# A hybrid decoder layer on one core: another order of seven-product and plain chunk pairs in its feed-forward parts, and padded pools

## The chip, the cores and the metric

One core of a Trainium2 chip runs the whole layer in one launch. The metric is the time of one execution on the device in microseconds. TensorE (PE) multiplies matrices, VectorE (DVE) and ScalarE (ACT) work elementwise, GpSimd (POOL) does little here, and SyncE (SP) issues the loads and stores. On-chip memory (SBUF) has 128 partitions; an address below is a byte offset within a partition. Matmul results go into eight accumulation banks (PSUM), each 512 float32 values wide per partition.

## The reference

The layer works on 256 tokens of width 2048 in float32:

```
x = x + 1/2 * SwiGLU_1(RMSNorm(x))            # 2048 -> 5632 -> 2048
h = RMSNorm(x); u = h @ W_in
x = x + W_out [ GLA_group(u) ; MoBA_group(u) ]
x = x + CrossAttn(RMSNorm(x), RMSNorm(mem))   # 4 heads, memory of 256
x = x + 1/2 * SwiGLU_2(RMSNorm(x))

def swiglu(h, w_gate, w_up, w_down):
    return (jax.nn.silu(h @ w_gate) * (h @ w_up)) @ w_down
```

The change concerns the gate and up products of the two SwiGLU parts, and where tiles lie.

## The kernel before

Every float32 operand is split into a high part in the matmul format and a rest (`split_to`, L151 to L153: ScalarE copies to `hi`, VectorE subtracts to `lo`). A product is then three matmuls into one bank (`mm3`, L163 to L167): high by high, high of the activations by rest of the weights, rest of the activations by high of the weights. The stationary operand is a 128x128 block of activations, the moving one 512 columns of weights. One such triple is called a product here.

The tokens make two tiles of 128 (t = 0, 1), the width 2048 makes 16 chunks of 128. The feed-forward width 5632 makes 11 column blocks of 512. `ffn` (L404) goes through them in groups of 4, 4 and 3 blocks; after each group a down stage multiplies what the group made with `w_down`, in four blocks of 512 output columns. Block 0 runs its gate and its up product one after the other (`Block`). All other blocks, 10 in each of the two feed-forward parts, run gate and up together as a `Pair` (from L197).

A pair takes the 16 chunks two by two, in eight steps. `KINDS` gives each step's kind. In an N step (plain) the two token tiles and the two weight matrices are multiplied with four products per chunk, 8 in all, or 24 matmuls: banks p2, q4, r3, r5 in that order, where r3 takes the difference of the two token tiles (tiles dh, dl). In an S step the two chunks, two token tiles and two matrices are treated as a 2x2 matrix product with seven products, or 21 matmuls, over combinations of activations (tiles eh, el, made once by `Normed.sums`) and of weights: VectorE first forms combinations of the weights (L232 wide, L234 and L235 narrow, tiles `st`), and these are split like the weights themselves. So an S step has four split tiles (two from `raw`, two from `st`) and an N step two. The split tiles `whi` and `wlo` have six buffers each (`HIS`), the raw weights three (`RAWS`, one buffer for a step of a pair).

All S steps also add to p1, r6 and r7, which no N step uses. After the last S step `early` (L246) reads those three. At a pair's end `gates` and `ups` read p2, q4, r5, r3 and r5 again, ScalarE applies the silu, VectorE multiplies (L449), and `turn` transposes the result on TensorE and splits it, pumped between the steps of what follows. The seven banks are taken by the next pair in the order p1, r6, r7, p2, r5, r3, q4.

The order of instructions on each engine is fixed when the kernel is built: a scheduler orders them by priority and readiness and places the waits, so neighbouring steps are interleaved. Each engine then runs its own queue in order.

Tiles come from pools laid one behind the other, with sizes in multiples of 32 bytes per partition: const, wp (raw), act (x, xhi, xlo, bighi, biglo), small, then the phase's tmp (whi, wlo, t2k, xg, st and others) and own (eh, el, dh, dl in the feed-forward phases; m_cum, m_tail, m_ch, s8d, go, s8a, s8b, s8c, s4a, decay, s4b in the mixer's). In small stand 13 tags of two 32-byte buffers each.

The first lines on the order of work at a pair's end:

```
for t, (g, u) in enumerate(zip(list(pair.gates()), list(pair.ups()))):
    r = a.rstd[:, t:t + 1]
    nc.scalar.activation(g, g, AF.Silu, scale=r)
    nc.vector.scalar_tensor_tensor(u, u, r, g, op0=ALU.mult, op1=ALU.mult)
```

Of the kernel before, what the change touches and what calls it, by code (L numbers as in the profile page):

```python
# [9 lines left out]
F32 = mybir.dt.float32  # L10
F32R = mybir.dt.float32r
BF16 = mybir.dt.bfloat16
AF = mybir.ActivationFunctionType
ALU = mybir.AluOpType
# [3 lines left out]
P = 128  # L18
# [4 lines left out]
KC = D // P  # L23
# [4 lines left out]
GH = 4  # L28
# [7 lines left out]
NCH = T // CH  # L36
# [9 lines left out]
RAWS = 3  # L46
HIS = 6
T2K = 7
KINDS = "SSSSNNNN"


@with_exitstack
def hymba_layer(ctx: ExitStack, tc: tile.TileContext, x, mem, ffn1_norm, ffn1_w_gate, ffn1_w_up,
# [3 lines left out]
    nc = tc.nc  # L57
# [6 lines left out]
    const = ctx.enter_context(tc.tile_pool(name="const", bufs=1))  # L64
    wp = ctx.enter_context(tc.tile_pool(name="wp", bufs=RAWS))
    act = ctx.enter_context(tc.tile_pool(name="act", bufs=1))
    small = ctx.enter_context(tc.tile_pool(name="small", bufs=2))
    pools = {}
# [13 lines left out]
    def nm(s):  # L82
        count[0] += 1
        return f"{s}_{count[0]}"
# [1 line left out]
    x_sb = act.tile([P, NT, D], F32, tag="x", name="x_sb")  # L86
    norms = [ffn1_norm, mix_norm, xattn_norm, mem_norm, ffn2_norm]
    G1, GMIX, GX, GMEM, G2 = range(5)
    graw = const.tile([KC, P], F32, name="graw")
    nc.sync.dma_start(x_sb[:, :, :NB], x[:, :NB].rearrange("(t p) n -> p t n", p=P))  # L90
    nc.sync.dma_start(graw, ffn1_norm.rearrange("o (c p) -> (o c) p", p=P))
    warm = small.tile([P, 1], F32, tag="mx", name="warm")
    nc.vector.memset(warm, 0.0)
    nc.scalar.activation(warm, warm, AF.Silu)
    ident = const.tile([P, P], F32, name="ident")
# [1 line left out]
    gT1 = const.tile([P, 32], F32, name="gT1")[:, :KC]  # L97
# [4 lines left out]
    def turn_gains(src, dst):  # L102
        n = src.shape[0]
        ps = aux_tile([P, NB])
        nc.tensor.transpose(ps[:, :n], src, ident[:n, :n])
        nc.vector.tensor_copy(dst, ps[:, :n])

    def aux_tile(shape):
        n = 1
        for s in shape[1:]:  # L110
            n *= s
        t = pools["aux"].tile([P, NB], F32, tag="aux", name=nm("aux"))[:, :n]
        if len(shape) == 3:
            t = t.rearrange("p (a b) -> p a b", a=shape[1])
        return t
# [4 lines left out]
    def own_tile(shape, tag, dtype=F32):  # L120
        return pools["own"].tile(shape, dtype, tag=tag, name=nm(tag))

    def tmp_tile(shape, tag, bufs=2, dtype=F32):
        return pools["tmp"].tile(shape, dtype, tag=tag, name=nm(tag), bufs=bufs)

    def half_kb(shape=(P, NB)):
        return tmp_tile(list(shape), "t2k", 8 if "mix" in pools else T2K)
# [27 lines left out]
    def split_raw(raw):  # L155

        k, n = raw.shape[1:]
        bufs = 3 if "mix" in pools else HIS
        hi, lo = (tmp_tile([P, 2, NB], tag, bufs, F32R)[:, :k, :n] for tag in ("whi", "wlo"))
        split_to(hi, lo, raw)  # L160
        return [(hi[:, i, :], lo[:, i, :]) for i in range(k)]
# [7 lines left out]
    def bank(n=NB):  # L169
        return pools["mm"].tile([P, NB], F32, tag="mm", name=nm("mm"))[:, :n]  # L170
# [26 lines left out]
    class Pair:  # L197
# [3 lines left out]
        def __init__(self, a, wg, wu, c0):  # L201
            self.a, self.wg, self.wu, self.c0 = a, wg, wu, c0
            self.p = {n: bank() for n in ("p1", "r6", "r7", "p2", "r5", "r3", "q4")}
            self.left = {n: KINDS.count("S") + (0 if n in ("p1", "r6", "r7") else 1) *
                         KINDS.count("N") for n in self.p}
            self.total = dict(self.left)
# [11 lines left out]
        def step(self, q):  # L218
# [4 lines left out]
            g, u2 = raw[:, 1:3], raw[:, 3:4]  # L223
            if KINDS[q] == "N":
                gs, us = split_raw(g), split_raw(raw[:, 0:4:3])
# [36 lines left out]
        def ups(self):  # L262

            c = self.v2
            nc.vector.tensor_tensor(c, self.p["r5"], c, op=ALU.add)  # L265
            nc.vector.tensor_tensor(c, self.p["r3"], c, op=ALU.add)
            yield c
            c = self.v3
            nc.vector.tensor_tensor(c, self.p["r5"], c, op=ALU.add)  # L269
            yield c  # L270
# [3 lines left out]
    def pump():  # L274

        while behind:
            try:
                next(behind[0])
                return
            except StopIteration:  # L280
                behind.popleft()
# [60 lines left out]
    class Normed:  # L342
# [6 lines left out]
        def begin(self):  # L349
            self.hi, self.lo = (act_tile([P, KC, T], tag, F32R) for tag in ("xhi", "xlo"))  # L350
            self.ss = small.tile([P, NT, 4], F32, tag="ss", name=nm("ss"))
            if self.pairs:
                self.s = [q for q in range(KC // 2) if KINDS[q] == "S"]
                self.n = [q for q in range(KC // 2) if KINDS[q] == "N"]
                self.e = [own_tile([P, len(self.s), 4, P], t, F32R) for t in ("eh", "el")]
# [13 lines left out]
        def sums(self, q, x):  # L369

            f = tmp_tile([P, 4, P], "xg", 3)
            if KINDS[q] == "S":
                for out, x0, x1 in ((f[:, 0], x[1][:, 0], x[1][:, 1]),
# [97 lines left out]
        phases.append(phase(name, n_mm))  # L471
        phases[0].__enter__()

    turn_gains(graw, gT1)
    n1 = Normed(G1, True)

    def load_x(j):
# [13 lines left out]
    n1.block(0)  # L491
    behind.append(start())
    pump()
    graw2 = const.tile([4 * KC + 4, P], F32, name="graw2")
    for i, g in enumerate(norms[1:]):
        nc.sync.dma_start(graw2[i * KC:(i + 1) * KC, :], g.rearrange("o (c p) -> (o c) p", p=P))
    for i, g in enumerate((moba_q_norm, moba_k_norm, xattn_q_norm, xattn_k_norm)):
# [19 lines left out]

    m_cum = pools["own"].tile([P, P], F32R, name="m_cum")
    m_tail = pools["own"].tile([P, P], F32R, name="m_tail")
    m_ch = pools["own"].tile([P, 2], F32R, name="m_ch")  # L520
    mask = tmp_tile([P, P], "at", 4)
    nc.gpsimd.memset(mask, 1.0 / TAU)
    nc.gpsimd.affine_select(out=mask, in_=mask, compare_op=ALU.is_ge, fill=0.0, base=0,
# [25 lines left out]
    rg = own_tile([P, NT, GW], "s8b")  # L549
    qkT = own_tile([P, 2, GH, T], "s8c")  # L550
    ktail = own_tile([P, NT, GQK], "s4a")
    decay = own_tile([P, GH, NCH], "decay")
    E = {}

    def scaled(dst, ps, rstd):
# [451 lines left out]
```

## Time and profile before

| what | value |
|---|---|
| median of 3 runs (lowest to highest) | 1985.28 us (1985.1 to 1986.78) |
| the profiled execution's own time | 1984.34 us |
| its span in the trace | 1982.6 us |
| TensorE busy, matmuls | 1945.7 us, 8872 |
| VectorE busy, instructions | 1489.4 us, 1832 |
| ScalarE busy, instructions | 1047.5 us, 1308 |
| DMA | 369.12 MB, 55.4% of 16 engines' span |

Busy time is the time in which at least one instruction of an engine is in progress. Matmuls overlap: one lasts some 390 ns by its record and the next starts before it ends, so the distance of two starts is what a matmul costs in a stream. In rows of instructions a name stands as line, engine, operation, what it writes and what it reads; brackets give the idle time before it and what ended it.

### The profile page before, as it was taken

To read this page: it belongs to the slowest core of one execution; us is meant where nothing else is said; L and a number is where in the kernel's file an instruction comes from. 1 tells how busy PE (TensorE), PEld (TensorE's weight loads), DVE (VectorE), ACT (ScalarE), POOL (GpSimd) and SP (SyncE) were. 2 spreads that over 40 slices of the span, in tenths; PEclk is the share of its full clock that TensorE was granted. 3 is DMA by queue.
4 is the path that set the end of the run, shared out by engine and by line. 5 is a ranking of instruction groups with operands and counts; after the bars stand their busy time and mean duration, and the time that the engine had idled before them with its cause. 6 is when DMAs were issued, how large, how long until landed. Compare 5 with 4: busy or idle time off the path is not lost.

```text
span 1982.6 us, 23399 instructions
## 1 busy us (share of the span) xinstructions
PE 1945.7 (98%) x8872; PEld 1590.8 (80%) x8872; DVE 1489.4 (75%) x1832; ACT 1047.5 (53%) x1308; POOL 23.5 (1%) x52
## 2 busy tenths in 40 slices
PE   7999999999999999999999999999999999999999
PEld 6877887778887788987788888887788777888777
DVE  8898579995699755465665766989857999569973
ACT  6555446554355545635464645655534655435552
POOL 0000000000000000000000000000000000000000
PEclk9999999999999999999999999999999999999999
DMA  7555555565555636554456545655554566555563
GB/s 255 191 191 191 192 169 191 195 213 200 177 186 186 223 129 207 164 191 149 150 169 205 178 149 167 196 198 183 192 199 161 191 206 213 196 170 191 191 213 127
DMA packets 192456, 369.12 MB, mean 186 GB/s; under 512 B 8692, under 2 KB 19144, under 8 KB 192344
## 3 DMA queue, kind: packets, MB, share of 16 engines
q1 hardware_dynamic: 192344, 367.64, 55.4%
q8 instruction: 69, 1.13, 0.2%
q14 instruction: 43, 0.35, 0.1%
HBM read 365.50 MB, written 2.10 MB: 185 GB/s over the span
## 4 chain that ended last, share of the span: by engine, by line
PE 77%; DVE 17%; ACT 3%; issue 2%; DMA 1%; SPq 0%; ACTq 0%
PE mm L165 24%; PE mm L167 24%; PE mm L166 24%; DVE wlo L153 8%; ACT whi L152 3%; DVE st L232 2%; DVE st L235 2%; DVE st L234 1%; DVE biglo L153 1%; DVE t2k L449 1%; PE aux L328 1%; DVE t2k L256 0%; DVE t2k L265 0%; DVE t2k L269 0%; DVE t2k L259 0%
## 5 line engine op out<-in xcount | busy, mean ns | idle before, releaser
L153 DVE TENSOR_TENSOR wlo<-raw,whi 128x1024 fp32r<-128x1024 f32 (+3 forms) x704 | 796.3, 1142 | 377.1 <-ACT whi L152 375.1
L152 ACT ACTIVATE whi<-raw 128x1024 fp32r<-128x1024 f32 (+3 forms) x704 | 683.5, 989 | 661.6 <-PE mm L167 561.1
L165 PE MATMUL mm<-whi,xhi 128*128 128x512 f32 (+2 forms) x1296 | 507.7, 392 | 1.0 <-ACT whi L152 1.0
L166 PE MATMUL mm<-wlo,xhi 128*128 128x512 f32 (+2 forms) x1296 | 502.7, 388 | 0.6 <-DVE wlo L153 0.5
L167 PE MATMUL mm<-whi,xlo 128*128 128x512 f32 (+2 forms) x1296 | 500.9, 387 | 0.0
L167 PE MATMUL mm<-whi,biglo 128*128 128x512 f32 x864 | 338.8, 392 | 0.1
L165 PE MATMUL mm<-whi,bighi 128*128 128x512 f32 x832 | 329.6, 396 | 0.0
L166 PE MATMUL mm<-wlo,bighi 128*128 128x512 f32 x832 | 324.1, 390 | 0.0
L167 PEld LDWEIGHTS mm<-whi,xlo 128*128 128x128 f32 x1296 | 243.7, 188 | 51.3 <-DVE xlo L153 1.1
L165 PEld LDWEIGHTS mm<-whi,xhi 128*128 128x128 f32 x1296 | 243.7, 188 | 50.9 <-ACT whi L152 1.9
L166 PEld LDWEIGHTS mm<-wlo,xhi 128*128 128x128 f32 x1296 | 244.1, 188 | 47.2 <-DVE wlo L153 2.2
L152 ACT ACTIVATE whi<-st 128x1024 fp32r<-128x1024 f32 x160 | 167.5, 1059 | 168.5 <-PE mm L167 78.9
L153 DVE TENSOR_TENSOR wlo<-st,whi 128x1024 fp32r<-128x1024 f32 x160 | 192.7, 1222 | 43.7 <-ACT whi L152 42.2
L167 PEld LDWEIGHTS mm<-whi,biglo 128*128 128x128 f32 x864 | 162.1, 188 | 37.7 <-DVE biglo L153 0.6
L166 PEld LDWEIGHTS mm<-wlo,bighi 128*128 128x128 f32 x832 | 156.3, 188 | 33.5
L165 PEld LDWEIGHTS mm<-whi,bighi 128*128 128x128 f32 x832 | 156.4, 188 | 31.2
L165 PE MATMUL mm<-whi,eh 128*128 128x512 f32 x320 | 122.7, 400 | 17.5 <-ACT whi L152 17.5
L166 PE MATMUL mm<-wlo,eh 128*128 128x512 f32 x320 | 125.5, 392 | 0.2
L167 PE MATMUL mm<-whi,el 128*128 128x512 f32 x320 | 125.1, 391 | 0.0
L232 DVE TENSOR_TENSOR st<-raw 128x1024 f32<-128x1024 f32 x80 | 97.6, 1220 | 1.2 <-DMA raw<-in_ffn_w_up_dram 0.5
L165 PEld LDWEIGHTS mm<-whi,eh 128*128 128x128 f32 x320 | 60.0, 188 | 41.9 <-ACT whi L152 30.0
L166 PEld LDWEIGHTS mm<-wlo,eh 128*128 128x128 f32 x320 | 60.1, 188 | 14.3 <-DVE wlo L153 1.9
(204 smaller groups left out, 1464.0 us busy)
## 6 DMA issues: line engine op xcount, KB each, us to landing
raw<-in_ffn_w_down_dram SPq DMA_DIRECT2D x88, 1024.0 KB, 5.1
raw<-in_ffn_w_gate_dram SPq DMA_DIRECT2D x162, 512.0 KB, 3.9
raw<-in_ffn_w_up_dram SPq DMA_DIRECT2D x160, 512.0 KB, 4.9
raw<-in_w_in_dram SPq DMA_DIRECT2D x40, 1024.0 KB, 5.1
raw<-in_w_out_dram SPq DMA_DIRECT2D x16, 1024.0 KB, 5.0
raw<-in_ffn_w_up_dram SPq DMA_DIRECT2D x8, 1024.0 KB, 5.3
raw<-in_ffn_w_gate_dram SPq DMA_DIRECT2D x7, 1024.0 KB, 6.1
raw<-in_w_in_dram SPq DMA_DIRECT2D x8, 688.0 KB, 4.1
```

Source lines behind the costliest of these rows:

```text
L152: nc.scalar.activation(hi, src, AF.Copy)
L153: nc.vector.tensor_tensor(lo, src, hi.bitcast(F32), op=ALU.subtract)
L165: nc.tensor.matmul(p, a[0], w[0], start=start, stop=False)
L166: nc.tensor.matmul(p, a[0], w[1], start=False, stop=False)
L167: nc.tensor.matmul(p, a[1], w[0], start=False, stop=stop)
L232: nc.vector.tensor_tensor(sa, raw[:, 1:4:2], raw[:, 0:1].to_broadcast([P, 2, NB]), op=ALU.add)
L234: nc.vector.tensor_tensor(sb[:, 0:1], sa[:, 0:1], u2, op=ALU.add)
L235: nc.vector.tensor_tensor(sb[:, 1, :], sb[:, 0, :], raw[:, 2, :], op=ALU.add)
L328: nc.tensor.transpose(pt[:, i, :], c[:, i * P:(i + 1) * P], ident)
L449: nc.vector.scalar_tensor_tensor(u, u, r, g, op0=ALU.mult, op1=ALU.mult)
```

## The change

`KINDS` goes from four S steps and then four N steps to N, S, N, S, N, S, N, N: three S steps and five N steps in each pair. In `ups` the bank r3 is read before r5. The tile `graw` is allocated with 128 partitions. `warm` gets a tag of its own of 192 bytes in the pool small, where it used the tag mx. `graw2` moves from the pool const into one of the t2k buffers of the first phase. In the mixer's pool own, m_ch goes from 8 to 512 bytes and decay from 64 to 512.

```
--- before.py
+++ after.py
@@ -46,7 +46,7 @@
 RAWS = 3
 HIS = 6
 T2K = 7
-KINDS = "SSSSNNNN"
+KINDS = "NSNSNSNN"
 
 
 @with_exitstack
@@ -86,10 +86,10 @@
     x_sb = act.tile([P, NT, D], F32, tag="x", name="x_sb")
     norms = [ffn1_norm, mix_norm, xattn_norm, mem_norm, ffn2_norm]
     G1, GMIX, GX, GMEM, G2 = range(5)
-    graw = const.tile([KC, P], F32, name="graw")
+    graw = const.tile([P, P], F32, name="graw")
     nc.sync.dma_start(x_sb[:, :, :NB], x[:, :NB].rearrange("(t p) n -> p t n", p=P))
-    nc.sync.dma_start(graw, ffn1_norm.rearrange("o (c p) -> (o c) p", p=P))
-    warm = small.tile([P, 1], F32, tag="mx", name="warm")
+    nc.sync.dma_start(graw[:KC, :], ffn1_norm.rearrange("o (c p) -> (o c) p", p=P))
+    warm = small.tile([P, 48], F32, tag="warm", name="warm", bufs=1)[:, :1]
     nc.vector.memset(warm, 0.0)
     nc.scalar.activation(warm, warm, AF.Silu)
     ident = const.tile([P, P], F32, name="ident")
@@ -262,8 +262,8 @@
         def ups(self):
 
             c = self.v2
+            nc.vector.tensor_tensor(c, self.p["r3"], c, op=ALU.add)
             nc.vector.tensor_tensor(c, self.p["r5"], c, op=ALU.add)
-            nc.vector.tensor_tensor(c, self.p["r3"], c, op=ALU.add)
             yield c
             c = self.v3
             nc.vector.tensor_tensor(c, self.p["r5"], c, op=ALU.add)
@@ -471,7 +471,7 @@
         phases.append(phase(name, n_mm))
         phases[0].__enter__()
 
-    turn_gains(graw, gT1)
+    turn_gains(graw[:KC, :], gT1)
     n1 = Normed(G1, True)
 
     def load_x(j):
@@ -491,7 +491,7 @@
     n1.block(0)
     behind.append(start())
     pump()
-    graw2 = const.tile([4 * KC + 4, P], F32, name="graw2")
+    graw2 = half_kb()[:4 * KC + 4, :P]
     for i, g in enumerate(norms[1:]):
         nc.sync.dma_start(graw2[i * KC:(i + 1) * KC, :], g.rearrange("o (c p) -> (o c) p", p=P))
     for i, g in enumerate((moba_q_norm, moba_k_norm, xattn_q_norm, xattn_k_norm)):
@@ -517,7 +517,7 @@
 
     m_cum = pools["own"].tile([P, P], F32R, name="m_cum")
     m_tail = pools["own"].tile([P, P], F32R, name="m_tail")
-    m_ch = pools["own"].tile([P, 2], F32R, name="m_ch")
+    m_ch = pools["own"].tile([P, P], F32R, name="m_ch")[:, :2]
     mask = tmp_tile([P, P], "at", 4)
     nc.gpsimd.memset(mask, 1.0 / TAU)
     nc.gpsimd.affine_select(out=mask, in_=mask, compare_op=ALU.is_ge, fill=0.0, base=0,
@@ -549,7 +549,7 @@
     rg = own_tile([P, NT, GW], "s8b")
     qkT = own_tile([P, 2, GH, T], "s8c")
     ktail = own_tile([P, NT, GQK], "s4a")
-    decay = own_tile([P, GH, NCH], "decay")
+    decay = own_tile([P, GH, P // GH], "decay")[:, :, :NCH]
     E = {}
 
     def scaled(dst, ps, rstd):
```

## Rows read from the trace of the kernel before

**Rows 1.** The page: span, TensorE, granted clock, chain by engine.

```profile
span 1982.6 us, 23399 instructions
...
PE 1945.7 (98%) x8872; PEld 1590.8 (80%) x8872; DVE 1489.4 (75%) x1832; ACT 1047.5 (53%) x1308; POOL 23.5 (1%) x52
...
PEclk9999999999999999999999999999999999999999
...
PE 77%; DVE 17%; ACT 3%; issue 2%; DMA 1%; SPq 0%; ACTq 0%
```

**Rows 2.** Windows, three pairs: from:to, us, then busy us (count) by engine.

```profile
63.09:105.53 42.44, 42.41 (x190) 34.43 (x189) 40.09 (x45) 25.45 (x29) 0.00 (x0) 1.00 0.60 198
282.33:323.74 41.41, 41.35 (x182) 33.72 (x180) 38.11 (x42) 24.53 (x27) 0.00 (x0) 1.00 0.62 204
...
367.74:411.74 44.00, 42.76 (x190) 34.44 (x188) 42.03 (x49) 25.68 (x29) 0.00 (x0) 1.00 0.56 191
```

**Rows 3.** VectorE by kind in the pair 367.74 to 411.74: busy us, mean ns.

```profile
L153 DVE TENSOR_TENSOR wlo<-raw,whi 128x1024 fp32r<-128x1024 f32 x13 | 15.6, 1222 | 0.4 <-ACT whi L152 0.3
L153 DVE TENSOR_TENSOR wlo<-st,whi 128x1024 fp32r<-128x1024 f32 x8 | 9.6, 1222 | 1.5 <-ACT whi L152 1.5
L232 DVE TENSOR_TENSOR st<-raw 128x1024 f32<-128x1024 f32 x4 | 4.9, 1220 | 0.0
```

**Rows 4.** Timeline of TensorE, 412 to 434: start, length, and idle before in brackets.

```profile
428.37 0.50 PE L165 MATMUL mm<-whi,eh 128*128 128x512 f32 x1 [0.45 <-ACT whi L152]
...
431.28 0.50 PE L165 MATMUL mm<-whi,eh 128*128 128x512 f32 x1 [0.80 <-ACT whi L152]
```

**Rows 5.** Timeline of ScalarE, 398 to 442.

```profile
427.25 1.06 ACT L152 ACTIVATE whi<-st 128x1024 fp32r<-128x1024 f32 x1 [1.59 <-DVE st L232]
```

**Rows 6.** Timeline of VectorE, 407 to 419, about the end of a pair.

```profile
408.75 0.69 DVE L256 TENSOR_TENSOR t2k<-mm,t2k 128x512 f32<-128x512 f32 x1
...
412.28 0.69 DVE L265 TENSOR_TENSOR t2k<-mm,t2k 128x512 f32<-128x512 f32 x1
...
413.48 0.69 DVE L266 TENSOR_TENSOR t2k<-mm,t2k 128x512 f32<-128x512 f32 x1
```

**Rows 7.** Timeline of TensorE, a down stage, first and last of 91 starts.

```profile
215.03 0.39 PE L165 MATMUL mm<-whi,bighi 128*128 128x512 f32 x1
...
235.63 0.39 PE L165 MATMUL mm<-whi,bighi 128*128 128x512 f32 x1
```

**Rows 8.** Timeline of TensorE, plain chunks: the starts of four runs.

```profile
442.02 0.40 PE L165 MATMUL mm<-whi,dh 128*128 128x512 f32 x1
...
443.40 0.39 PE L165 MATMUL mm<-whi,xhi 128*128 128x512 f32 x1
...
447.52 0.39 PE L165 MATMUL mm<-whi,dh 128*128 128x512 f32 x1
...
448.88 0.39 PE L165 MATMUL mm<-whi,xhi 128*128 128x512 f32 x1
```

**Rows 9.** Timeline of TensorE, first S chunk of a pair.

```profile
413.11 0.39 PE L165 MATMUL mm<-whi,eh 128*128 128x512 f32 x1
...
415.83 0.39 PE L165 MATMUL mm<-whi,xhi 128*128 128x512 f32 x1
...
417.20 0.40 PE L166 MATMUL mm<-wlo,xhi 128*128 128x512 f32 x1
```

**Rows 10.** Timeline of TensorE, memory projection, first and last of 31 starts.

```profile
1158.49 0.40 PE L165 MATMUL mm<-whi,s8b 128*128 128x512 f32 x1
...
1165.49 0.40 PE L165 MATMUL mm<-whi,s8c 128*128 128x512 f32 x1
```

**Rows 11.** The page, costliest groups: first products of xhi and bighi.

```profile
L165 PE MATMUL mm<-whi,xhi 128*128 128x512 f32 (+2 forms) x1296 | 507.7, 392 | 1.0 <-ACT whi L152 1.0
...
L165 PE MATMUL mm<-whi,bighi 128*128 128x512 f32 x832 | 329.6, 396 | 0.0
```

**Rows 12.** Timeline of TensorE, 409 to 412: r3 of the last chunk begins.

```profile
409.00 0.39 PE L165 MATMUL mm<-whi,dh 128*128 128x512 f32 x1
```

More of the change, by code (lines that the diff above doesn't have):

```diff
@@ L48 @@
 T2K = 7
-KINDS = "SSSSNNNN"
+KINDS = "NSNSNSNN"
 @with_exitstack
@@ L88, in hymba_layer @@
     G1, GMIX, GX, GMEM, G2 = range(5)
-    graw = const.tile([KC, P], F32, name="graw")
+    graw = const.tile([P, P], F32, name="graw")
     nc.sync.dma_start(x_sb[:, :, :NB], x[:, :NB].rearrange("(t p) n -> p t n", p=P))
-    nc.sync.dma_start(graw, ffn1_norm.rearrange("o (c p) -> (o c) p", p=P))
-    warm = small.tile([P, 1], F32, tag="mx", name="warm")
+    nc.sync.dma_start(graw[:KC, :], ffn1_norm.rearrange("o (c p) -> (o c) p", p=P))
+    warm = small.tile([P, 48], F32, tag="warm", name="warm", bufs=1)[:, :1]
     nc.vector.memset(warm, 0.0)
@@ L264, in ups @@
             c = self.v2
+            nc.vector.tensor_tensor(c, self.p["r3"], c, op=ALU.add)
             nc.vector.tensor_tensor(c, self.p["r5"], c, op=ALU.add)
-            nc.vector.tensor_tensor(c, self.p["r3"], c, op=ALU.add)
             yield c
@@ L472, in next_phase @@
         phases[0].__enter__()
-    turn_gains(graw, gT1)
+    turn_gains(graw[:KC, :], gT1)
     n1 = Normed(G1, True)
@@ L493, in hymba_layer @@
     pump()
-    graw2 = const.tile([4 * KC + 4, P], F32, name="graw2")
+    graw2 = half_kb()[:4 * KC + 4, :P]
     for i, g in enumerate(norms[1:]):
@@ L519, in hymba_layer @@
     m_tail = pools["own"].tile([P, P], F32R, name="m_tail")
-    m_ch = pools["own"].tile([P, 2], F32R, name="m_ch")
+    m_ch = pools["own"].tile([P, P], F32R, name="m_ch")[:, :2]
     mask = tmp_tile([P, P], "at", 4)
@@ L551, in hymba_layer @@
     ktail = own_tile([P, NT, GQK], "s4a")
-    decay = own_tile([P, GH, NCH], "decay")
+    decay = own_tile([P, GH, P // GH], "decay")[:, :, :NCH]
     E = {}
```

## The prediction

> **What bounds the kernel now.** I read the page first: TensorE is busy 1945.7 of 1982.6 us, the chain that ended last is matmuls for 77% and VectorE for 17%, and the granted clock stands at the top step (2.4 GHz) in every slice [rows 1]. A busy share of 98% is an overlap of matmul records of 390 ns that start every 227 to 233 ns, so it cannot show whether the stream is at its best. So I went on with two questions: how long is one pair of gate and up blocks against its count of matmuls, and what is the spacing of the matmuls where nothing waits.
>
> A pair that follows another takes 44.00 us for 180 matmuls of 512 columns and 8 transposes; one that follows the plain blocks at the start takes 42.44, one that follows a down stage 41.41, without transposes [rows 2]. The code gives 14, 2 and 4 of these (its groups of 3, 4 and 3 pairs, twice). VectorE is busy 42.03 us of the 44.00 [rows 2]. By kind, a seven-product chunk (S) costs it one wide sum, two narrow ones, three wide splits and one narrow: 1.22 + 2 x 0.69 + 3 x 1.22 + 0.69 = 6.95 us, a plain chunk (N) two wide splits, 2.44 us (the wide ones by [rows 3], the narrow by those of 512 columns in [rows 6]). TensorE needs 21 x 0.229 = 4.8 us for S and 24 x 0.229 = 5.5 us for N. So four S in a row ask VectorE for 27.8 us while TensorE eats them in 19.2, and the lead in the six split buffers runs out: TensorE waits 0.45 and 0.80 us for a split on ScalarE, always in the third and fourth S chunk [rows 4], and that split waited 1.59 us for VectorE's sum [rows 5]. In the N half VectorE idles. That is the cover which the new order uses.
>
> **The change, part by part.**
>
> *One S chunk becomes N.* Three more matmuls in each of 20 pairs. They stand on TensorE's path: 60 x 0.227 = +13.6 us.
>
> *Taking turns.* Work of VectorE in a pair falls by 6.95 - 2.44 to 37.5 us, against some 42.4 us of TensorE: 88% busy instead of 96%. An N and an S chunk together ask for 9.4 us (8.9 when back-to-back instructions overlap their ends) and TensorE takes 10.3 us, so VectorE keeps up from each N to the next S. With six buffers and 2 + 4 per N and S, each split tile takes the place of the same tile one turn earlier; the last of an S chunk comes free at that chunk's end and is wanted again 5.5 + 3.4 us later, with 2.3 us of split to do. From the last S of a pair to the first S of the next lie three N chunks, 16.4 us, which hold the pair's ends (two early, two gates, three ups, two products, two turns: 11 instructions of 0.69 us), 7.6 us, beside 3 x 2.44 us of splits and 6.95 of the S chunk. That is 21.9 us against 16.4 + 4.8 + 0.9 of transposes = 22.1 on TensorE: the tightest place. I take 0.2 us of wait left in each pair: bounds are 0 and the 1.25 us of today [rows 4]. If the cover fails there, the price is that 1.25 us per pair, 25 us.
>
> *Order of bank reads.* Bank r3 is complete 1.4 us before the pair ends, r5 only at the end. Today the reads of r5 start at 412.28 and r3 is read last, at 413.48 [rows 6]. In the new order a pair begins with an N chunk, which wants p2 at once, q4 after 1.4 us, r3 after 2.7 and r5 after 4.1. p2 is read at 408.75, 3 us before the end at 411.74 [rows 2, 6]; r3 can now be read before the end; r5's second read would end some 2 us after it, 2 us before it is wanted. Cost 0; it lies beside 4.1 us of other banks' matmuls. On VectorE the splits of the next chunks stand behind these reads, which is in the sum above.
>
> *Places modulo 512 bytes.* By the sizes in the code, weights' splits (whi, wlo) now begin 320 bytes off the grid on which xhi, xlo, bighi and biglo lie: the 13 small tags of 64 bytes make 832. The combinations eh, el, dh, dl come out of the same grid as whi; the mixer's s8 tiles lie 32 bytes off whi, behind the mask of 8 bytes. After the change (832 + 192 = 1024; the mask and decay 512 each) all lie alike. What that may be worth shows already. Unlike by 320: 90 matmuls of the down stage in 20.60 us, 228.9 ns each [rows 7], and 18 from xhi in 4.12 us, 228.9 [rows 8]. Alike: six from dh in 1.36 us, 226.7 [rows 8], twelve from eh in 2.72 us, 226.7 [rows 9]. Off by 32: 30 in 7.00 us, 233.3 [rows 10]. Three places, three spacings, wherever in the kernel. So I take 226.7 for all. VectorE gains nothing: a wide split from raw (unlike whi) and one from st (alike) take 1222 ns both [rows 3].
>
> The Trainium skill, "SBUF — State Buffer", section "Who interferes with whom", says that TensorE has two read ports of its own, for moving data and for weights, and never waits on anyone. By that rule the place of a tile is worth nothing. The three spacings speak against it, but a place with all tiles alike has run here only in short stretches; the first rival is what it would leave.
>
> *The rest.* graw, warm: same work. graw2 takes one of seven t2k slots until its transpose; the first block uses four beside it, so nothing waits. Its eight loads stay where they are in SP's queue. The norm's sums for one chunk get shorter on VectorE, beside matmuls: 0, at most 1 us.
>
> **The sum**, on the profiled execution. A full pair after: 183 x 0.2267 + 2 x 0.46 of transposes (in 415.83 to 417.20 stand four matmuls and one group of them, 1.37 - 4 x 0.2289 [rows 9]) = 42.4 us; without transposes 41.5. Gains: 14 x (44.00 - 42.4) = 22.4; 2 x 0; 4 x (41.4 - 41.5) = -0.4. So the pairs give 22.0, the 13.6 already in. Other matmuls: first products from xhi and bighi are 1296 + 832 [rows 11], 36 x 20 = 720 of them in pairs, so 1408 x 3 x 2.2 ns = 9.3 us, and 288 from s8, of which 96 with 512 columns at 6.6 ns: 0.6. Less 20 x 0.2 = 4 us of waits. 22.0 + 9.3 + 0.6 - 4 = 28 us. The profiled execution took 1984.34 us, its span 1982.6, the median of the runs 1985.28, 0.9 above it: I forecast 1957.
>
> **Rivals.**
>
> *Places are worth nothing* (0.20). All matmuls stay at 228.9 ns. A full pair is 183 x 0.2289 + 0.92 = 42.8: 14 x 1.2 - 2 x 0.4 - 4 x 0.5 = 14, less 4 of waits: 10 us, 1975. For it: one of the two stretches from dh took 1.38 us for six, 230 ns, though alike [rows 8]; it follows the S half, where TensorE had waited. Against: three levels by place. The Trainium skill's rule above says the same as this rival.
>
> *The waits move* (0.13). VectorE's order is fixed when the kernel is built; one S chunk per pair still comes late, say the first, behind the pair's ends, and costs today's 1.25 us. 28 + 4 - 25 = 7 us: 1978. For it: the 21.9 against 22.1 us above leave hardly any slack. Against: that count gives VectorE no lead at its start and no overlap of instruction ends; it has both.
>
> *The new beginning of a pair stalls TensorE: slower* (0.05). Today a pair begins with p1, whose bank was read early in the pair before; now with p2, read only by the gates at 408.75 [rows 6], 1.1 us after its last matmul (p2's six ended one bank's 1.4 us ahead of 409.00, where r3's begin [rows 12]). If the gates' reads get queued on VectorE behind the splits and sums of the next S chunk, TensorE stands still at every pair's start. Price: what they start later than 411.05 us on this scale (the pair's end less one read). It outweighs the gain of 32 us when it passes 1.6 us per pair, with a start 3.9 us later than today's; behind a whole S chunk of 6.95 us it would be 4.65 us x 20 = 93 less 32: 61 us slower, 2046. Against it: VectorE now has slack at that point, and there the next S is a chunk further off.
>
> **How the numbers follow.** Forecast 0.62, with a range of its own of 1950 (no wait left, an equal start) to 1965 (half of the gain by place). The rivals 0.20, 0.13, 0.05. The range for 8 in 10 goes from 1947 to 1978, which takes in both smaller gains. A measurement of this kernel tells 0.2%, 4 us, from no change. Faster by more holds in the forecast and in most of the first two rivals: 0.88; within it 0.06, where waits move and places are worth nothing at once; slower 0.06.
>
> **What would show it.** Right: pairs at 42.4 to 42.8 us in the timeline, VectorE busy near 37.5 in each, no idle of TensorE on a split in the S chunks, matmuls from xhi and bighi 226.7 ns apart. If they are still 228.9 apart, places failed. If TensorE idles before the first matmul from p2's bank, or before an S chunk, the turns failed; the releaser tells which. Wrong altogether: pairs at 44 us or more.

## The result, and the profile after

The changed kernel takes 1957.01 us (median of 4, 1955.91 to 1957.72) against 1985.19 us before: a ratio of 0.9856, with a 95% interval from 0.9839 to 0.9873. The forecast was 1957 with a range of 1947 to 1978.

Lines of the page after the change, those that answer to [rows 1] and [rows 11]:

```profile
span 1954.2 us, 23322 instructions
...
PE 1933.9 (99%) x8932; PEld 1604.1 (82%) x8932; DVE 1410.2 (72%) x1726; ACT 1019.8 (52%) x1268; POOL 23.8 (1%) x52
...
PE 97%; DVE 1%; DMA 1%; ACT 0%; issue 0%; SPq 0%
...
L165 PE MATMUL mm<-whi,xhi 128*128 128x512 f32 (+2 forms) x1356 | 528.0, 390 | 1.2 <-ACT whi L152 1.2
...
L165 PE MATMUL mm<-whi,bighi 128*128 128x512 f32 x832 | 326.3, 392 | 0.0
```

The span is 28.4 us shorter although there are 60 matmuls more (8932). VectorE's 17% of the chain [rows 1] are 1% now: the chain is matmuls from end to end. The first products from xhi are 60 more, 3 for each pair.

Three pairs after the change, in the columns of [rows 2] (from:to, us, then busy us and count of TensorE, its weight loads, VectorE, ScalarE, GpSimd, then clock, DMA share and GB/s): the first pair, one that follows a down stage, one that follows a pair:

```profile
62.60:105.06 42.46, 42.46 (x193) 35.13 (x192) 36.41 (x40) 24.27 (x27) 0.00 (x0) 1.00 0.59 198
277.96:319.44 41.48, 41.48 (x185) 34.35 (x184) 35.24 (x38) 23.30 (x25) 0.00 (x0) 1.00 0.56 189
361.88:404.33 42.45, 42.45 (x193) 35.13 (x191) 37.86 (x43) 24.27 (x27) 0.00 (x0) 1.00 0.59 201
```

A pair that follows another takes 42.45 us instead of 44.00, and TensorE is busy in all of it. The starts of the matmuls give the same for 16 pairs (42.45 to 42.46) and 41.48 for each of the four that follow a down stage. The 20 pairs together take 845.1 us against 866.3 before: 21.2 us of the 28.4. The other 7.2 lie outside the pairs.

VectorE in the third of these pairs, as in [rows 3]:

```profile
L153 DVE TENSOR_TENSOR wlo<-raw,whi 128x1024 fp32r<-128x1024 f32 x13 | 15.7, 1219 | 3.1 <-ACT whi L152 3.1
L153 DVE TENSOR_TENSOR wlo<-st,whi 128x1024 fp32r<-128x1024 f32 x6 | 7.3, 1220 | 0.6 <-ACT whi L152 0.5
L232 DVE TENSOR_TENSOR st<-raw 128x1024 f32<-128x1024 f32 x3 | 3.7, 1220 | 0.6 <-DMA raw<-in_ffn_w_up_dram 0.6
```

Two splits of sums and one wide sum fewer, as an S chunk less must give, and the same 1220 ns each: the new places changed nothing for VectorE. In all it is busy 37.86 us of 42.45; forecast were 37.5.

Starts on TensorE, to be held against [rows 7 to 10]. A down stage, 90 matmuls apart; a plain chunk, 18 matmuls from xhi and then 6 from dh; the memory projection, 30 apart:

```profile
210.64 0.39 PE L165 MATMUL mm<-whi,bighi 128*128 128x512 f32 x1
...
231.04 0.39 PE L165 MATMUL mm<-whi,bighi 128*128 128x512 f32 x1
```

```profile
402.97 0.39 PE L165 MATMUL mm<-whi,xhi 128*128 128x512 f32 x1
...
407.05 0.39 PE L165 MATMUL mm<-whi,dh 128*128 128x512 f32 x1
...
408.41 0.39 PE L165 MATMUL mm<-whi,xhi 128*128 128x512 f32 x1
```

```profile
1143.05 0.39 PE L165 MATMUL mm<-whi,s8b 128*128 128x512 f32 x1
...
1149.85 0.39 PE L165 MATMUL mm<-whi,s8c 128*128 128x512 f32 x1
```

20.40, 4.08, 1.36 and 6.80 us: 226.7 ns in every one of them, where 228.9, 228.9, 226.7 to 230 and 233.3 stood before.

The reads of banks at the end of that pair (it ends at 404.33), on VectorE, as in [rows 6]:

```profile
400.63 0.68 DVE L256 TENSOR_TENSOR t2k<-mm,t2k 128x512 f32<-128x512 f32 x1
...
404.20 0.68 DVE L265 TENSOR_TENSOR t2k<-mm,t2k 128x512 f32<-128x512 f32 x1
...
405.94 0.68 DVE L266 TENSOR_TENSOR t2k<-mm,t2k 128x512 f32<-128x512 f32 x1
406.54 0.68 DVE L269 TENSOR_TENSOR t2k<-mm,t2k 128x512 f32<-128x512 f32 x1
```

p2 is read 3.7 us before the end, r3 at the end, r5 1.6 and 2.2 us behind it.

### The profile page after: what moved, and what is told of

It reads as the page before. It is cut to its first block, busy times and chain, and to the rows that moved or that the text cites. A ratio compares the mean times of both kernels' runs of the same rounds, so it can differ in the third digit from the quotient of the medians.

```text
span 1954.2 us, 23322 instructions
## 1 busy us (share of the span) xinstructions
PE 1933.9 (99%) x8932; PEld 1604.1 (82%) x8932; DVE 1410.2 (72%) x1726; ACT 1019.8 (52%) x1268; POOL 23.8 (1%) x52
## 4 chain that ended last, share of the span: by engine, by line
PE 97%; DVE 1%; DMA 1%; ACT 0%; issue 0%; SPq 0%
PE mm L165 31%; PE mm L167 31%; PE mm L166 31%; PE aux L415 1%; PE aux L328 1%; DVE wlo L153 0%; DMA raw<-in_xattn_w_o_dram 0%; PE aux L746 0%; DMA raw<-in_ffn_w_gate_dram 0%; ACT whi L152 0%; PE aux L696 0%; PE aux L691 0%; PE aux L667 0%; PE aux L932 0%; PE aux L781 0%
## 5 line engine op out<-in xcount | busy, mean ns | idle before, releaser
L165 PE MATMUL mm<-whi,xhi 128*128 128x512 f32 (+2 forms) x1356 | 528.0, 390 | 1.2 <-ACT whi L152 1.2
L167 PE MATMUL mm<-whi,xlo 128*128 128x512 f32 (+2 forms) x1356 | 522.2, 385 | 0.0
L153 DVE TENSOR_TENSOR wlo<-st,whi 128x1024 fp32r<-128x1024 f32 x120 | 146.6, 1222 | 30.3 <-ACT whi L152 26.8
L152 ACT ACTIVATE whi<-st 128x1024 fp32r<-128x1024 f32 x120 | 127.2, 1060 | 66.0 <-PE mm L167 43.4
L165 PE MATMUL mm<-whi,eh 128*128 128x512 f32 x240 | 93.4, 389 | 0.0
L167 PE MATMUL mm<-whi,el 128*128 128x512 f32 x240 | 93.4, 389 | 0.0
L166 PE MATMUL mm<-wlo,eh 128*128 128x512 f32 x240 | 93.4, 389 | 0.0
L232 DVE TENSOR_TENSOR st<-raw 128x1024 f32<-128x1024 f32 x60 | 73.2, 1220 | 7.0 <-DMA raw<-in_ffn_w_up_dram 6.3
L165 PE MATMUL mm<-whi,dh 128*128 128x512 f32 x200 | 77.8, 389 | 0.0
L166 PE MATMUL mm<-wlo,dh 128*128 128x512 f32 x200 | 77.8, 389 | 0.0
```

The lines of the kernel that those rows point to most:

```text
L152: nc.scalar.activation(hi, src, AF.Copy)
L153: nc.vector.tensor_tensor(lo, src, hi.bitcast(F32), op=ALU.subtract)
L165: nc.tensor.matmul(p, a[0], w[0], start=start, stop=False)
L166: nc.tensor.matmul(p, a[0], w[1], start=False, stop=False)
L167: nc.tensor.matmul(p, a[1], w[0], start=False, stop=stop)
L232: nc.vector.tensor_tensor(sa, raw[:, 1:4:2], raw[:, 0:1].to_broadcast([P, 2, NB]), op=ALU.add)
```

## The experiments

All are held against the kernel before in the same session; the ratio's 95% interval stands in brackets. Two questions were open: which share the new `KINDS` and the places each have, and whether it is the number of S chunks or their turns that frees VectorE.

**1. The new KINDS without the places.**

```
-KINDS = "SSSSNNNN"          # kernel before, nothing else changed
+KINDS = "NSNSNSNN"
```

> The kernel before with the new order of kinds alone; pools and the order of bank reads as before. Theory (two separate gains): matmuls from xhi and bighi stay 228.9 ns apart, a full pair takes 183 x 0.2289 + 0.92 = 42.8 us with no wait on a split, 14 us less in all than before: 1971 us. Rival A (the turns bring everything, places nothing): the time of the changed kernel, 1957. Rival B (the old order of bank reads stalls a pair that begins with an N chunk): TensorE idle in front of r3's first matmul, 0.5 to 1.2 us per pair, 1981 to 1995.

1969.4 us, 0.9915 [0.990 to 0.993]. A pair that follows another, and first and last of 91 starts in a down stage:

```profile
364.76:407.45 42.69, 42.69 (x192) 35.15 (x191) 38.15 (x43) 24.29 (x27) 0.00 (x0) 1.00 0.59 197
```

```profile
213.03 0.39 PE L165 MATMUL mm<-whi,bighi 128*128 128x512 f32 x1
...
233.63 0.39 PE L165 MATMUL mm<-whi,bighi 128*128 128x512 f32 x1
```

The pair is 42.69 us long, TensorE is busy throughout, and the 90 matmuls still take 20.60 us. So the waits on splits are gone by the new `KINDS` alone, which has both one S chunk less and the turns (experiments 5 and 6 part the two), and the spacing is not touched by it. Rival A falls, as places bring the rest, and so does rival B: no wait stands at a pair's beginning with the old order of bank reads.

**2. The places without the new KINDS.**

```
-KINDS = "NSNSNSNN"          # changed kernel, and r5 read before r3 again
+KINDS = "SSSSNNNN"
```

> The changed kernel with four S and then four N chunks and the old order of bank reads: only the places are new. Theory: outside the pairs the gain measured after the change, 7.3 us; in the S half of a pair VectorE sets the pace, so that half stays as long and TensorE waits longer; in the N half 96 matmuls x 2.2 ns = 0.2 us per pair, 4 us: in all 11 us, 1974. Waits on splits per full pair grow from 1.8 to above 2 us. Rival (places bring nothing): 1985, spacing 228.9.

1973.47 us, 0.9938 [0.9923 to 0.9952]. A pair, TensorE's waits in it, and a down stage:

```profile
366.59:410.26 43.67, 42.39 (x190) 34.41 (x188) 41.83 (x49) 25.66 (x29) 0.00 (x0) 1.00 0.57 193
```

```profile
383.18 0.50 PE L165 MATMUL mm<-whi,eh 128*128 128x512 f32 x1 [0.50 <-ACT whi L152]
...
386.10 0.50 PE L165 MATMUL mm<-whi,eh 128*128 128x512 f32 x1 [0.78 <-ACT whi L152]
```

```profile
215.68 0.39 PE L165 MATMUL mm<-whi,bighi 128*128 128x512 f32 x1
...
236.08 0.39 PE L165 MATMUL mm<-whi,bighi 128*128 128x512 f32 x1
```

Both waits of [rows 4] are there, in the same places, 0.50 and 0.78 us. The matmuls of the down stage are 226.7 ns apart. The pair is 0.33 us shorter than before, not the 0.2 expected: 0.25 in its N half and 0.08 in its S half, by the starts. TensorE's idle time in a pair goes from 1.25 to 1.29 us; the growth to above 2 us that was expected did not come. The new `KINDS` alone gives 16.3 us, places alone 12.3, both 28.2: they add up within 0.4 us.

**3. The order of bank reads.**

```
 c = self.v2                 # changed kernel
-nc.vector.tensor_tensor(c, self.p["r3"], c, op=ALU.add)
 nc.vector.tensor_tensor(c, self.p["r5"], c, op=ALU.add)
+nc.vector.tensor_tensor(c, self.p["r3"], c, op=ALU.add)
```

> The changed kernel with r5 read before r3 again. Theory (the order of bank reads lies beside 2.7 us of other banks' matmuls): 1957 within 4 us, no wait at a pair's beginning. Rival: r3 comes free too late, TensorE waits ahead of r3's first matmul in each pair, 0.3 to 1.2 us x 20: 1963 to 1981.

1957.17 us, 0.9854 [0.9839 to 0.9868]: no difference. A pair, then VectorE's read of r3 and TensorE's first matmul into the next pair's r3, just behind it:

```profile
363.20:405.65 42.45, 42.45 (x193) 35.13 (x191) 38.06 (x43) 24.27 (x27) 0.00 (x0) 1.00 0.60 199
```

```profile
407.98 0.68 DVE L266 TENSOR_TENSOR t2k<-mm,t2k 128x512 f32<-128x512 f32 x1
```

```profile
408.37 0.39 PE L165 MATMUL mm<-whi,dh 128*128 128x512 f32 x1
```

The time was forecast, but for another reason than the one given. The next pair's r3 starts at 408.37, while the old r3 is still being read until 408.66: the two cannot lie in the same bank. In the program as built the next pair's p2, q4 and r3 lie in the three banks which p1, r6 and r7 had, read long before by `early`. The read of the old r3 therefore frees nothing that the next pair's r3 wants: a name need not get the same bank again.

**4. The weights' splits 32 bytes off.**

```
-warm = small.tile([P, 48], F32, tag="warm", name="warm", bufs=1)[:, :1]
+warm = small.tile([P, 40], F32, tag="warm", name="warm", bufs=1)[:, :1]
```

> The changed kernel with warm of 160 instead of 192 bytes, so that all weights' splits and all tiles behind them lie 32 bytes ahead of the grid of xhi, xlo, bighi and biglo; the work is the same. Theory (the distance of the stationary from the moving tile modulo 512 bytes sets the spacing, as with the s8 tiles before): matmuls from xhi and bighi 233.3 ns apart, those from eh and dh 226.7; (1356 + 832) x 3 x 6.6 ns = 43 us more, 2000. Rival A (any unlikeness costs 2.2 ns): 1957 + 14 = 1971. Rival B (places have nothing to do with it): 1957.

1996.07 us, 1.0048 [1.0031 to 1.0064]: slower than the kernel before, for a pad 32 bytes shorter. 90 matmuls of a down stage:

```profile
218.98 0.40 PE L165 MATMUL mm<-whi,bighi 128*128 128x512 f32 x1
...
239.98 0.40 PE L165 MATMUL mm<-whi,bighi 128*128 128x512 f32 x1
```

21.00 us, 233.3 ns each: the spacing of the s8 tiles before [rows 10], brought about on purpose in other tiles. Against the changed kernel 39 us are lost, 43 were expected. Runs of six from dh and of twelve from eh, which moved along with the splits and were expected at 226.7 ns, took 230.2 and 227.6 ns on average between their unlike neighbours. So the place is the cause, and not the stage, the height of the address or the tile. By the rule of the Trainium skill that the prediction weighed ("SBUF — State Buffer", "Who interferes with whom"), TensorE waits on nobody and this edit would cost nothing; these rows decide against that reading of it.

**5. Three S chunks, in front.**

```
-KINDS = "NSNSNSNN"
+KINDS = "SSSNNNNN"
```

> The changed kernel with its three S chunks at the front of a pair (S S S N N N N N): VectorE's work per pair is the same 37.5 us, only the turns are gone. Theory (the turns matter, not the count alone: each S chunk asks VectorE for 2.15 us more than TensorE takes, and the lead of six buffers covers about two of them): a wait of 0.5 to 1.0 us in the third S chunk of the 16 pairs that follow others, 8 to 16 us, 1965 to 1973. Rival (the count alone does it, VectorE at 88% is enough wherever the S chunks stand): 1957, no wait on a split.

1959.19 us, 0.9868 [0.9853 to 0.9883]. A pair:

```profile
364.08:406.63 42.55, 42.55 (x192) 35.05 (x191) 37.93 (x43) 24.11 (x27) 0.00 (x0) 1.00 0.59 198
```

42.55 us, 0.10 more than in turns. By the starts one matmul of the third S chunk comes 0.08 us late in such a pair, and that is all. The theory fell here: the expected wait of 0.5 to 1.0 us is not there. With three S chunks the lead of the buffers nearly suffices, and turns bring 1.4 us in the 20 pairs (846.5 against 845.1); the two ratios' intervals overlap.

**6. Four S chunks, in turns.**

```
-KINDS = "NSNSNSNN"
+KINDS = "NSNSNSNS"
```

> The changed kernel with four S chunks in turns (N S N S N S N S): 180 matmuls per pair again. TensorE needs 180 x 0.2267 + 0.92 = 41.7 us, VectorE 42.0. Theory (the one that is busier sets the pace): pairs of 42.0 to 42.9 us, VectorE busy near 98% in a pair, waits back on TensorE; 1948 to 1966, no clear difference from the changed kernel. Rival (turns alone hide all of VectorE's work, the count of S is free): 41.7 us per pair, 1942.

1944.05 us, 0.9788 [0.9772 to 0.9805]: 13 us faster than the changed kernel. Two pairs, a usual one and the longest:

```profile
361.58:403.32 41.74, 41.74 (x189) 34.53 (x188) 41.56 (x48) 25.69 (x29) 0.00 (x0) 1.00 0.61 203
317.88:361.58 43.70, 42.59 (x189) 34.33 (x188) 43.30 (x50) 25.73 (x29) 0.00 (x0) 1.00 0.59 194
```

41.74 us with TensorE busy throughout: the rival was right, and four S chunks are free if they take turns. VectorE is busy 41.56 us of them, so nothing is left over. The long pair shows what that costs. In the pair before it VectorE waited three times for loads of weights, 5.7 us in all, and was late with the read of r6 in `early` (L250), which now falls at the pair's end. The last of these waits, and the read:

```profile
313.22 1.23 DVE L232 TENSOR_TENSOR st<-raw 128x1024 f32<-128x1024 f32 x1 [1.17 <-DMA raw<-in_ffn_w_up_dram]
...
319.70 0.68 DVE L250 TENSOR_TENSOR t2k<-mm,t2k 128x512 f32<-128x512 f32 x1
```

```profile
320.44 0.50 PE L165 MATMUL mm<-whi,xhi 128*128 128x512 f32 x1 [1.04 <-DVE t2k L250]
```

The read starts 1.8 us behind the pair's end (317.88); in the other pairs it starts at most 0.6 us behind it. TensorE stood 1.04 us for it: the matmul that waited is the first into the next pair's q4, so q4 got r6's bank, as experiment 3 has it. Three of the 20 pairs are 0.5 us or more too long in this execution, the longest of the four (1946.25 us).

**7. Other distances.** A pad of 448, 384 and 256 bytes at the front of the pools tmp of the three phases puts the splits 64, 128 and 256 bytes ahead of the grid of xhi, xlo, bighi and biglo. Lines are two higher in this kernel.

```
 pools.update(mm=mm, aux=aux, tmp=tmp, own=own)
+shift = tmp.tile([P, {"a": 112, "b": 96, "c": 64}[name]], F32, tag="pad", ...)
+nc.gpsimd.memset(shift[:, :1], 0.0)
```

> The changed kernel with a pad at the front of each phase's pool tmp, so that the weights' splits begin 64, 128 and 256 bytes ahead of the grid of the activations in the three phases (first feed-forward part, mixer and memory read, second feed-forward part). A look at the spacing in three stages. Theory (the distance modulo 512 sets it, and 0 is the only free one): spacings between 229 and 233.3 ns from xhi and bighi in each stage, a level of its own for each distance; from eh, dh and the mixer's s8 tiles, which move along with the splits, 226.7. Rival (only 32 bytes and 320 bytes cost something, for another reason): 226.7 in at least two of the three.

One execution, 1978.72 us. Starts in the three phases: 90 apart at 64 bytes, 42 apart at 128 bytes, 90 apart at 256 bytes:

```profile
220.28 0.39 PE L167 MATMUL mm<-whi,bighi 128*128 128x512 f32 x1
...
241.28 0.39 PE L167 MATMUL mm<-whi,bighi 128*128 128x512 f32 x1
```

```profile
1113.59 0.39 PE L167 MATMUL mm<-whi,bighi 128*128 128x512 f32 x1
...
1123.35 0.39 PE L167 MATMUL mm<-whi,bighi 128*128 128x512 f32 x1
```

```profile
1460.13 0.39 PE L167 MATMUL mm<-whi,bighi 128*128 128x512 f32 x1
...
1480.53 0.39 PE L167 MATMUL mm<-whi,bighi 128*128 128x512 f32 x1
```

21.00, 9.76 and 20.40 us: 233.3, 232.4 and 226.7 ns. The theory was right that 64 and 128 bytes cost something and wrong for 256 bytes, which cost nothing; nor has every distance a level of its own, for 64 bytes cost what 32 did in experiment 4. The rival falls with two stages of three above 226.7. Runs from dh and eh, which move along with the splits, took 229.8 and 228.9 ns in the first phase, not 226.7, and 226.7 in the third.

**8. Four S chunks in turns, with an N at the end.**

```
-KINDS = "NSNSNSNN"
+KINDS = "SNSNSNSN"
```

> The changed kernel with four S chunks in turns that begin with an S and end with an N (S N S N S N S N). With N S N S N S N S a late load let TensorE wait 1.04 us for the early read of a bank (one pair of 43.7 us in place of 41.8), because there the last S ends the pair and the banks p1, r6 and r7 are read only at its end. Theory: with the last chunk an N that read lies 5 us ahead of the pair's end, TensorE does not wait for it, every pair that follows another takes 41.8 us, the span is some 3 us shorter than the four in turns that ended on S: 1941 us. Rival A (VectorE at 99% is the cause, wherever its late work falls): waits of 0.4 to 1.9 us turn up on splits instead, 1944. Rival B (the first chunk S meets the pair's ends on VectorE, as before the change): 0.5 us and more per pair, 1951 or above.

1943.47 us, 0.9796 [0.9783 to 0.9810]. A pair:

```profile
359.46:401.23 41.77, 41.77 (x189) 34.57 (x188) 41.56 (x48) 25.49 (x30) 0.00 (x0) 1.00 0.63 204
```

All 16 pairs with transposes take 41.77 us in this execution, the other four 40.80, and no long one is among them; the span is 1941.6 us against 1944.5 in experiment 6, whose profiled execution was its longest. In these two executions the mechanism behaves as the theory has it. The medians, 1943.47 and 1944.05, don't tell the two orders apart. Either is the fastest version here, some 13 us ahead of the changed kernel and 41 ahead of the one before.

The four cells side by side, all with the new places:

| | four S | three S |
|---|---|---|
| in front | 1973.5 us | 1959.2 us |
| in turns | 1944.1 us (1943.5 with N last) | 1957.0 us |

## Why the prediction was right, point by point

- *What bounds the kernel.* Right: the waits of [rows 4] were what the turns took away (experiment 1), and VectorE's lead was their cause: the same waits stand in experiment 2, whatever the spacing.
- *One S chunk becomes N, +13.6 us.* Right in size: the count of S is worth 13 us in turns (1957.0 against 1944.1). But it was priced as what the gain needs, and it isn't. In turns, four S leave no wait either (experiment 8). The sum took "less work for VectorE" and "turns" as one step; the table shows that each of them nearly does it alone, and that the change pays for both. A cheaper way to the same end stood in the rows, and the prediction did not price it: the expectation of experiment 6 still took 42.0 us of VectorE against 41.7 of TensorE as VectorE's bound, while back to back VectorE does that work in 41.6.
- *Taking turns, 0.2 us of wait left per pair.* Mis-sized: no wait is left in any pair, so 4 us of allowance were too much.
- *A full pair, 42.4 us.* Measured 42.45, and 41.48 for 41.5. The pairs gave 21.2 us, for 22.0 less the 4 us of allowance.
- *Order of bank reads, 0.* Right in size (experiment 3), wrong in its reason: banks were taken to keep their names from pair to pair. They don't, so the read order had no bank to free in time. The third rival, slower by the new beginning of a pair, rested on the same error. Its mechanism is real where the last chunk is an S (experiment 6), but there it is `early` that is late, not the gates.
- *Places, 226.7 ns for all.* Right, and shown both ways: 12.3 us by places alone (experiment 2), 39 us lost by a shift of 32 bytes (experiment 4). The first rival falls. Its pair of 42.8 us was also too long: it charged 2.2 ns to all 183 matmuls, though those from dh and eh lay alike already, and experiment 1 measured 42.69. That the grid has 512 bytes isn't needed: 256 bytes off is as good as none (experiment 7).
- *Other matmuls, 9.9 us.* Mis-sized: 7.2 measured. A down stage of 384 matmuls got 0.8 us shorter, as 2.1 ns each must make it. Most of what is missing lies in the stretch from the last down stage of the first feed-forward part to the second part's first pair, which got only 3.0 us shorter, from 627.05 to 624.06 us. Two things held it back, by the starts. The narrow matmuls gained nothing there: 190 of 344 columns lie 156.5 ns apart before and 157.2 after, and 182 of 256 columns lie 123.9 and 125.2 apart. For 288 of the narrow ones the 2.2 ns had been counted as well, 0.6 us. And the 1954 matmuls of 512 columns from xhi, xlo, bighi and biglo that follow directly on one another gained 1.5 ns each and not 2.2: they take 450.8 us instead of 453.8. Why they gained less than in the down stages no run here settles.

The allowance was 4 us too cautious, the other matmuls 2.7 us and the pairs 0.8 us too hopeful. These errors nearly cancel: the mechanism was right, but that the forecast hit to the microsecond is luck.

## What to carry to other kernels

Where one kind of step overtaxes a helper engine and another leaves it idle, put them in turns before you make fewer of the dear ones: compare the two engines' work over the whole cycle, not over the half in which one falls behind. Measure the distance of two starts, not the busy share, in streams of matmuls; if equal matmuls have different distances in different stages, look at where their stationary and moving tiles lie. And check which buffer a name gets the next time before you reason on who frees it.

## What the runs showed of the hardware that I had not expected

The spacing of float32 matmuls of 512 columns depends on the distance of the stationary tile from the moving one, in bytes within a partition: 226.7 ns at 0 and at 256, 233.3 at 32 and at 64, 232.4 at 128, and 228.9 at 192, counted modulo 512 from the moving to the stationary tile. All are at a granted clock of 1.00 (2.4 GHz). That 0 and 256 agree fits a period of 256 bytes, but no other two distances were run that would test it.

228.9 is the mean of unequal distances. In the down stages of the kernel before, the three matmuls of a product start 232, 226 and 229 ns ahead of the next one (medians); at 32 bytes (experiment 4) all three lie at 233 to 234, and after the change all three at 227. So the distance in bytes is not all that counts. And alike is not best for every width: the median of the 182 distances of matmuls of 256 columns from the s8 tiles is 118 ns before, at 32 bytes, and 120 after, at 0.

What in the chip makes the difference is not settled by these runs; distances between these steps and other widths were not tried on purpose.
